# Token-major projections: 512 columns at a time and a bank per token tile, in place of 256 columns and a bank per pair of tiles

## The chip, the cores and the metric

The kernel runs on one core of a Trainium2 chip. The metric is the time of one execution on the device, in microseconds (us); a kernel's time is the median of several runs. PE is the matrix engine, DVE the vector engine, ACT the scalar engine, SP the engine that issues most of the loads, and PEld PE's weight loads. PSUM, where PE writes, has eight banks of 128 partitions x 512 fp32.

## The reference, cut to what matters

Two layers of a block over 256 context tokens and 256 image tokens (512 in all), model width 1024. Each layer projects the normalized input into many parts, mixes them in three branches, and ends in a convolutional FFN. The last layer needs only the image tokens, except in keys and values. The parts that the change touches:

```python
# every layer, h is the normalized, modulated input [tokens, 1024]
q_x = rope_axial(rms_norm(bq_x.reshape(b, n, 4, 2, 64), q_norm_g), ang_r, ang_c)   # 512 columns
k_x = rope_axial(rms_norm(bk_x ...), ang_r, ang_c)                                 # 512 columns
k_c = rms_norm(bk_c ...)                                                           # context: no rotation
v   = bv                                                                           # 512 columns

def spatial_gating(u, v, norm_g, w_s, b_s):                                        # sv: 512 columns
    u = gelu(u)
    v = rms_norm(gelu(v).reshape(b, n // 128, 128, 4, 128), norm_g)
    mixed = einsum('gij,bnjgc->bnigc', w_s, v) + b_s.T[:, :, None]
    return u * mixed.reshape(b, n, 512)
```

Beside them stands a gated delta rule (a triangular solve per chunk of 64 tokens and a scan over the chunks), softmax attention with the difference of two maps, three gated branch products and the FFN.

## The kernel before, in words

Products are made from fp32 operands split in two (`hh`/`hl` for the input, `wh`/`wl` for the weights): three matmuls per 128 rows of the contraction. Most projections are feature-major (`proj_fm`): weights stationary, 512 tokens (256 in layer 1) streaming. Four are token-major (`proj_tm`, line 706): 128 tokens of the input are stationary and the weights' columns stream, so the tokens land on the partitions, where norms over a head's columns are a reduction along the free axis. These four are attention's v, k and q and the gate's sv.

In `proj_tm` each of the four has two groups of 256 columns. A PSUM bank holds a pair of token tiles, 256 columns each. Two banks of tag "p" hold the two pairs of 512 tokens; in layer 1, q and the gate work on the image tokens alone, one pair. For each of two weight blocks (512 KB: 512 contraction rows x 256 columns, line 711) the loop goes over pairs, the two tiles of a pair, four steps of the contraction and three matmuls. Then `use` runs for every pair.

`use_qk` (line 755) reads a pair out of PSUM with ACT (`axq`), squares it (`asq`), sums the squares per head on DVE (`qkss`), takes a reciprocal root in nine small DVE steps (`rsqrt`, line 242), multiplies by the gain or, for image tokens, by the cosines, and adds the swapped halves times the sines (four small multiplications, line 776), multiplies k by its root, transposes four 128x128 blocks on PE into a bank of tag "a" (`pqkT`, line 789) and copies the result to `kT` or `qT` with ACT. `axq`, `asq` and `axc` share three buffers of tag "ta". `sgu`'s `use` (line 676) does Gelu, square, sum and root, and leaves the mixing product (`mix`, line 687) to be issued later, by `flush` in the next projection. `v` is only copied.

PSUM banks by tag: "p" 2, "g" 3, "a" 2, "b" 1. Weights are loaded by SP into three buffers `wr` of 512 KB, split by ACT (`wh`) and DVE (`wl`) into four buffers each of 128x512. `more` (line 478) takes one step of the modulation vectors of later stages: a 512 KB load into a single buffer `wmt` and, in layer 0, two products with a running sum on DVE (line 471). Layer 0's `attn_project` takes one such step ahead of each of its six groups.

The order of instructions on each engine is fixed when the kernel is built, by a planner: it goes through time with its own costs and gives each engine the ready instruction of highest priority, which is program order, except that work under `high_priority` goes ahead of the rest. So the delta rule's keys, solve, intra products and scan (lines 579 to 587), and in layer 0 the `use` of q and k, go ahead of matmuls that are only there to be done; these fill PE between them. Each engine then runs its own list in order. Buffers and banks of a tag go to its tiles in the order of the program.

In `mixer` (line 574) the order is: delta rule's q, k, v and gates; its keys; the solve (`gdn_solve`, line 1149: 31 steps of two dependent DVE operations, `sT` and `sL`, then products on PE, `pZ` and `pU`, and ACT's copies into `U`); `attn_project`; the scan; `sgu`; z; the attention core; the branches.

Of the kernel before, what the change touches and what calls it, by code (L numbers as in the profile page):

```python
# [14 lines left out]
AF = mybir.ActivationFunctionType  # L15
ALU = mybir.AluOpType
# [3 lines left out]
L = 2  # L20
# [75 lines left out]
def host_layout(i):  # L96
    i = {k: np.asarray(v) for k, v in i.items()}
    f = np.ascontiguousarray
    o = {}
# [7 lines left out]
    w = i["w_in"]  # L107
# [38 lines left out]
    for name, key in (("alog", "a_log"), ("dtb", "dt_bias")):  # L146
        a = i[key]
# [26 lines left out]
class _Kernel:  # L174
# [488 lines left out]
    def sgu(self):  # L663
        nc, l, c0 = self.nc, self.l, self.c0
        gu = self.slot(10, "gu", [128, 4, NT])
        for m in range(4):
            p = self.bank("p", "pu")
            self.proj_fm(self.a["wfm"][l, 16 + m], 8, self.hh, self.hl, c0, p)
            self.more(l == 0)
            self.act(gu[:, m, c0:], p[:, :NT - c0], AF.Gelu_apprx_tanh)  # L670
        wb = self.tp.tile([128, 2, 4, 128], F32, tag="gS", name="sguwb", bufs=1)
        wT, bs = wb[:, 0], wb[:, 1]
        nc.scalar.dma_start(out=wT, in_=self.a["sguw"][l])
        nc.scalar.dma_start(out=bs, in_=self.a["sgub"][l].rearrange("p (g i) -> p g i", g=4))

        def use(gr, t0, p):
            gv = self.tmp("gv", [128, 2, 2, 128])
            self.act(gv, p.rearrange("p (t g c) -> p t g c", t=2, g=2), AF.Gelu_apprx_tanh)
            sq = self.tmp("gsq", [128, 2, 2, 128])
            self.act(sq, gv, AF.Square)  # L680
            ss = self.small("gss", [128, 2, 2], bufs=2)
            nc.vector.tensor_reduce(out=ss, in_=sq, axis=AX.X, op=ALU.add)
            self.rsqrt(ss, ss, 1.0 / 128, EPS, "s")
            self.mul(gv, gv, ss.unsqueeze(3).to_broadcast([128, 2, 2, 128]))
            self.late.append(lambda: mix(gr, t0, gv))

        def mix(gr, t0, gv):
            pm = self.bank("g", "pmix")
            pv = pm.rearrange("p (g t i) -> p g t i", g=2, t=2)
            for t in range(2):  # L690
                for g in range(2):
                    self.mm(pv[:, g, t], gv[:, t, g, :], wT[:, 2 * gr + g, :])
            for g in range(2):
                G = 2 * gr + g
                mx = self.tmp("mx", [128, 2, 128])
                self.stt(mx, pv[:, g], self.P(l, "sg", G), bs[:, G].unsqueeze(1).to_broadcast([128, 2, 128]),
                         ALU.mult, ALU.add)
                d = gu[:, G, t0 * 128:t0 * 128 + 256].rearrange("p (t i) -> p t i", t=2)
                self.mul(d, d, mx)

        for gr in range(2):
            self.proj_tm(6 + gr, c0, lambda t0, p, gr=gr: use(gr, t0, p))
        self.dump(f"ya{l}", gu)
        return gu

    def proj_tm(self, g, c0, use, ahead=False):

        pairs = range(c0 // 256, 2)
        pt = {i: self.bank("p", f"ptm{i}") for i in pairs}
        for kb in range(2):  # L710
            wh, wl = self.wblock(self.a["wtm"][self.l, g, kb].rearrange("p k m -> p (k m)"), 1024, 512)
# [12 lines left out]
        with ExitStack() as es:  # L724
            if ahead:
                es.enter_context(self.tc.high_priority(offset=AHEAD))
            for i in pairs:
                use(2 * i, pt[i])

    def flush(self):  # L730

# [4 lines left out]
    def attn_project(self):  # L736
        nc, l, c0 = self.nc, self.l, self.c0
        tabs = {}
        for nm in ("q", "k"):
            g = self.P(l, nm + "g")  # L740
            ct = self.small(f"ct{nm}", [128, 2, 64])
            st = self.small(f"st{nm}", [128, 2, 64])
# [12 lines left out]
        def use_qk(nm, dstT, gr):  # L755
            g, ct, st = tabs[nm]

            def use(t0, p):
                p8 = self.tmp("axq", [128, 2, 4, 64], tag="ta", bufs=3)
                self.act(p8, p.rearrange("p (t h d) -> p t h d", t=2, d=64), AF.Copy)  # L760
                sq = self.tmp("asq", [128, 2, 4, 64], tag="ta", bufs=3)
                self.act(sq, p8, AF.Square)
                ss = self.small("qkss", [128, 2, 4], bufs=2)
                nc.vector.tensor_reduce(out=ss, in_=sq, axis=AX.X, op=ALU.add)
                rs = self.small("qkrs", [128, 2, 4], bufs=2)
                self.rsqrt(rs, ss, 1.0 / 64, EPS, "q")
                xc = self.tmp("axc", [128, 2, 4, 64], tag="ta", bufs=3)
                if t0 == 0:
                    self.mul(xc, p8, g.unsqueeze(1).unsqueeze(1).to_broadcast([128, 2, 4, 64]))
                else:  # L770
                    xs = sq
                    self.mul(xc, p8, ct.unsqueeze(2).to_broadcast([128, 2, 4, 64]))
                    p5 = p8.rearrange("p t h (a b f) -> p t h a b f", a=2, b=2, f=16)
                    x5 = xs.rearrange("p t h (a b f) -> p t h a b f", a=2, b=2)
                    s5 = st.rearrange("p t (a b f) -> p t a b f", a=2, b=2)
                    for t in range(2):
                        for b in range(2):
                            self.mul(x5[:, t, :, :, b, :], p5[:, t, :, :, 1 - b, :],
                                     s5[:, t, :, b, :].unsqueeze(1).to_broadcast([128, 4, 2, 16]))
                    self.add(xc, xc, xs)  # L780
                if nm == "k":
                    self.mul(xc, xc, rs.unsqueeze(3).to_broadcast([128, 2, 4, 64]))
                else:
                    nc.vector.tensor_scalar_mul(self.qscale[:, t0:t0 + 2, 4 * gr:4 * gr + 4], rs, 0.125)
                pt = self.bank("a", "pqkT")
                pv = pt.rearrange("p (h t) -> p h t", h=2)
                for h in range(2):
                    for t in range(2):
                        nc.tensor.transpose(pv[:, h, 128 * t:128 * t + 128],
                                            xc[:, t, 2 * h:2 * h + 2, :].rearrange("p m d -> p (m d)"),  # L790
                                            self.C("ident"))
                self.act(dstT[:, 2 * gr:2 * gr + 2, 128 * t0:128 * t0 + 256], pv, AF.Copy)

            return use

        def one(w):
            gr = w % 2
            if w < 2:
                self.proj_tm(w, 0, use_qk("k", kT, gr), l == 0)
            elif w < 4:  # L800
                self.proj_tm(w, 0, lambda t0, p, gr=gr: self.act(
                    vB[:, t0:t0 + 2, 256 * gr:256 * gr + 256], p.rearrange("p (t c) -> p t c", t=2), AF.Copy))
            else:
                self.proj_tm(w, c0, use_qk("q", qT, gr), l == 0)
# [580 lines left out]
```

## Time and profile before

| | |
|---|---|
| median of 3 runs | 1648.79 us (1646.63 to 1651.72) |
| the profiled execution | 1647.11 us, span 1645.3 us |
| PE busy | 1585.5 us (96%) |
| DVE busy | 1201.7 us (73%) |
| ACT busy | 763.0 us (46%) |
| granted PE clock, mean | 0.982 |

The profile is that of one execution. The span runs from the first to the last instruction; busy time of PE includes the overlap of matmuls in its pipeline. The chain of work that ended last goes back from the last instruction to what released it, step by step; a long unbroken run of matmuls in it shows how far apart their starts are.

### The profile page before, as it was taken

To read this page: it belongs to the slowest core of one execution; us is meant where nothing else is said; L and a number is where in the kernel's file an instruction comes from. 1 tells how busy PE (TensorE), PEld (TensorE's weight loads), DVE (VectorE), ACT (ScalarE), POOL (GpSimd) and SP (SyncE) were. 2 spreads that over 40 slices of the span, in tenths; PEclk is the share of its full clock that TensorE was granted. 3 is DMA by queue.
4 is the path that set the end of the run, shared out by engine and by line. 5 is a ranking of instruction groups with operands and counts; after the bars stand their busy time and mean duration, and the time that the engine had idled before them with its cause. 6 is when DMAs were issued, how large, how long until landed. Compare 5 with 4: busy or idle time off the path is not lost.

```text
span 1645.3 us, 27181 instructions
## 1 busy us (share of the span) xinstructions
PE 1585.5 (96%) x10478; PEld 1339.4 (81%) x10478; DVE 1201.7 (73%) x2793; ACT 763.0 (46%) x1451; POOL 6.6 (0%) x16
## 2 busy tenths in 40 slices
PE   5999999999999998999999998999999999989999
PEld 3778977876788886888788887788878799989999
DVE  5648977788764456888778886659767866788685
ACT  3644461156532333544224442664723764566564
POOL 0000000000000000000000000000000000000000
PEclk9989999999999999999999999999999999999999
DMA  8413311142343433355556665222222246645655
GB/s 335 135 54 105 118 65 52 64 122 73 99 145 96 148 96 97 116 160 161 173 185 200 196 200 201 66 90 56 75 65 78 93 130 218 191 141 180 191 181 154
DMA packets 65282, 218.21 MB, mean 133 GB/s; under 512 B 7552, under 2 KB 13696, under 8 KB 63232
## 3 DMA queue, kind: packets, MB, share of 16 engines
q1 hardware_dynamic: 63280, 208.70, 40.2%
q10 hardware_dynamic: 1872, 7.77, 1.3%
q8 instruction: 82, 1.34, 0.3%
q14 instruction: 48, 0.39, 0.1%
HBM read 213.29 MB, written 3.15 MB: 132 GB/s over the span
## 4 chain that ended last, share of the span: by engine, by line
PE 78%; DVE 9%; DMA 4%; ACT 4%; issue 3%; ACTq 0%; DVEq 0%
PE pup L240 16%; PE pg L240 12%; PE pdn L240 11%; PE pqkv L240 8%; PE pbr L240 6%; PE pwo L240 4%; PE ptm L240 4%; DMA wmt<-in_wmt_dram 3%; PE pu L240 2%; PE psc L240 2%; PE pj L240 2%; PE pS L240 2%; ACT U L237 1%; PE pkS L240 1%; PE po L240 1%
## 5 line engine op out<-in xcount | busy, mean ns | idle before, releaser
L237 ACT ACTIVATE wh<-wr 128x512 fp32r<-128x512 f32 (+1 forms) x594 | 365.6, 621 | 411.2 <-PE pdn L240 84.1
L219 DVE TENSOR_TENSOR wl<-wr,wh 128x512 fp32r<-128x512 f32 (+1 forms) x592 | 399.2, 680 | 155.8 <-ACT wh L237 153.0
L240 PE MATMUL pup<-hh,wh 128*128 128x512 f32 (+1 forms) x704 | 238.4, 339 | 3.0 <-ACT hh L237 2.8
L240 PE MATMUL pup<-hh,wl 128*128 128x512 f32 (+1 forms) x704 | 238.2, 338 | 0.0
L240 PE MATMUL pup<-hl,wh 128*128 128x512 f32 (+1 forms) x704 | 237.4, 338 | 0.0
L240 PEld LDWEIGHTS pup<-hh,wh 128*128 128x128 f32 x704 | 134.9, 192 | 18.0 <-ACT hh L237 3.4
L240 PEld LDWEIGHTS pup<-hh,wl 128*128 128x128 f32 x704 | 134.9, 192 | 13.8
L240 PEld LDWEIGHTS pup<-hl,wh 128*128 128x128 f32 x704 | 134.6, 192 | 14.1
L240 PE MATMUL pg<-hh,wh 128*128 128x512 f32 (+1 forms) x384 | 131.0, 341 | 0.1
L240 PE MATMUL pg<-hh,wl 128*128 128x512 f32 (+1 forms) x384 | 130.4, 340 | 0.1
L240 PE MATMUL ptm<-wh,hl 128*128 128x256 f32 x448 | 130.4, 291 | 0.0
L240 PE MATMUL pg<-hl,wh 128*128 128x512 f32 (+1 forms) x384 | 130.3, 339 | 0.0
L240 PE MATMUL ptm<-wl,hh 128*128 128x256 f32 x448 | 129.9, 290 | 0.3 <-DVE wl L219 0.3
L240 PE MATMUL ptm<-wh,hh 128*128 128x256 f32 x448 | 129.6, 289 | 0.0
L471 DVE SCALAR_TENSOR_TENSOR wmt<-wmt,scb 128x1024 f32<-128x1024 f32 x80 | 97.6, 1220 | 34.0 <-DMA wmt<-in_wmt_dram 33.6
L234 DVE SCALAR_TENSOR_TENSOR fcv<-pup,par,fcv 128x510 f32<-128x510 f32 (+1 forms) x176 | 107.3, 611 | 18.5 <-ACT fcv L237 18.4
L240 PE MATMUL pdn<-fl,wh 128*128 128x512 f32 (+1 forms) x352 | 118.1, 336 | 1.2 <-DVE fl L219 1.2
L240 PE MATMUL pdn<-fh,wh 128*128 128x512 f32 (+1 forms) x352 | 118.6, 337 | 0.7 <-ACT fh L237 0.7
L240 PE MATMUL pdn<-fh,wl 128*128 128x512 f32 (+1 forms) x352 | 118.3, 336 | 0.0
L240 PEld LDWEIGHTS ptm<-wl,hh 128*128 128x128 f32 x448 | 86.7, 194 | 2.5 <-issue 1.7
L240 PEld LDWEIGHTS ptm<-wh,hh 128*128 128x128 f32 x448 | 86.5, 193 | 2.7 <-issue 2.0
L240 PEld LDWEIGHTS ptm<-wh,hl 128*128 128x128 f32 x448 | 86.6, 193 | 2.1 <-issue 1.7
(332 smaller groups left out, 3182.0 us busy)
## 6 DMA issues: line engine op xcount, KB each, us to landing
wmt<-in_wmt_dram SPq DMA_DIRECT2D x80, 512.0 KB, 3.6
wr<-in_wup_dram SPq DMA_DIRECT2D x80, 512.0 KB, 3.9
wr<-in_wfm_dram SPq DMA_DIRECT2D x78, 512.0 KB, 3.6
wr<-in_wtm_dram SPq DMA_DIRECT2D x32, 512.0 KB, 3.6
wr<-in_wdn_dram SPq DMA_DIRECT2D x32, 512.0 KB, 4.0
wr<-in_wbr_dram SPq DMA_DIRECT2D x24, 512.0 KB, 3.6
wm<-in_wmod_dram SPq DMA_DIRECT2D x8, 1024.0 KB, 10.9
wr<-in_wo_dram SPq DMA_DIRECT2D x16, 512.0 KB, 3.8
```

What stands on the lines that cost most here:

```text
L219: self.nc.vector.tensor_tensor(out=out, in0=a, in1=b, op=op)
L234: self.nc.vector.scalar_tensor_tensor(out=out, in0=a, scalar=s, in1=b, op0=op0, op1=op1)
L237: self.nc.scalar.activation(out, a, f, bias=bias, scale=scale, **k)
L240: self.nc.tensor.matmul(out, lhsT, rhs, start=start, stop=stop, **k)
L471: nc.vector.scalar_tensor_tensor(out=o, in0=w, scalar=1.0, in1=sb[:, v], op0=ALU.mult, op1=ALU.mult, accum_out=m4[:, n % 4, v:v + 1])
```

## The change

`proj_tm` takes all 512 columns of a projection at once: four groups in a layer instead of eight, each matmul 512 columns wide, a bank per tile of 128 tokens. With four tiles, tiles 0 and 1 take the banks of "p", tiles 2 and 3 those of "a"; with two tiles, both take "p" or both "a", by a counter. The weights are laid out anew: a block of 512 KB holds 256 contraction rows x 512 columns, so there are four blocks in a group. `use` runs per token tile, on 512 columns of one tile instead of 256 columns of two. The transposes of q and k go to the bank of tag "b". The gate's normed values of all tiles are kept, and a mixing product is issued for every second tile. The squares of the gate take a buffer of tag "tg". Layer 0's six modulation steps come in pairs ahead of the three groups v, k, q.

```diff
-    o["wtm"] = f(tm.reshape(L, 2, 4, 128, 8, 256).transpose(0, 4, 1, 3, 2, 5))
+    o["wtm"] = f(tm.reshape(L, 4, 2, 128, 4, 512).transpose(0, 4, 1, 3, 2, 5))
...
+    def two(self, name):
+        return [self.bank("a", name) for _ in range(2)]
...
-        def use(gr, t0, p):
-            gv = self.tmp("gv", [128, 2, 2, 128])
...
+        gvs = {}
+
+        def use(t, p):
+            gvs[t] = gv = self.tmp("gv", [128, 4, 128])
...
+            sq = self.tmp("gsq", [128, 4, 128], tag="tg", bufs=4)
...
-            self.late.append(lambda: mix(gr, t0, gv))
+            if t % 2:
+                self.late.append(lambda: mix(t - 1))
...
-        for gr in range(2):
-            self.proj_tm(6 + gr, c0, lambda t0, p, gr=gr: use(gr, t0, p))
+        self.proj_tm(3, c0, use)
...
-        pairs = range(c0 // 256, 2)
-        pt = {i: self.bank("p", f"ptm{i}") for i in pairs}
-        for kb in range(2):
+        ts = range(c0 // 128, 4)
+        self.alt += 1
+        pt = {}
+        for t in ts:
+            if len(ts) == 4 and t >= 2 or len(ts) == 2 and self.alt % 2:
+                if t == 2:
+                    pa = self.two("ptm")
+                pt[t] = pa[t - 2]
+            else:
+                pt[t] = self.bank("p", "ptm")
+        for kb in range(4):
             wh, wl = self.wblock(self.a["wtm"][self.l, g, kb].rearrange("p k m -> p (k m)"), 1024, 512)
-            for i in pairs:
-                for tt in range(2):
-                    o = pt[i][:, 256 * tt:256 * tt + 256]
-                    xs = slice((2 * i + tt) * 128, (2 * i + tt) * 128 + 128)
-                    for kk in range(4):
-                        k = kb * 4 + kk
-                        j, ws = kk // 2, slice(kk % 2 * 256, kk % 2 * 256 + 256)
-                        f = k == 0 and tt == 0
-                        self.mm(o, self.hh[:, k, xs], wh[j][:, ws], start=f, stop=False, skip_group_check=True)
-                        self.mm(o, self.hl[:, k, xs], wh[j][:, ws], start=False, stop=False, skip_group_check=True)
-                        self.mm(o, self.hh[:, k, xs], wl[j][:, ws], start=False, stop=k == 7, skip_group_check=True)
+            for t in ts:
+                xs = slice(128 * t, 128 * t + 128)
+                for kk in range(2):
+                    k = kb * 2 + kk
+                    self.mm(pt[t], self.hh[:, k, xs], wh[kk], start=k == 0, stop=False)
+                    self.mm(pt[t], self.hl[:, k, xs], wh[kk], start=False, stop=False)
+                    self.mm(pt[t], self.hh[:, k, xs], wl[kk], start=False, stop=k == 7)
...
-                    for t in range(2):
-                        for b in range(2):
-                            self.mul(x5[:, t, :, :, b, :], p5[:, t, :, :, 1 - b, :],
-                                     s5[:, t, :, b, :].unsqueeze(1).to_broadcast([128, 4, 2, 16]))
+                    for b in range(2):
+                        self.mul(x5[:, :, :, b, :], p5[:, :, :, 1 - b, :],
+                                 s5[:, :, b, :].unsqueeze(1).to_broadcast([128, 8, 2, 16]))
...
-                pt = self.bank("a", "pqkT")
...
+                pt = self.bank("b", "pqkT")
...
-        for w in (2, 0, 3, 1, 4, 5):
-            self.more(l == 0)
+        for w in (1, 0, 2):
             one(w)
```

In `one`, layer 0 now begins with `self.more(2)`; group 1 is v, 0 is k, 2 is q.

## Rows read from the trace of the kernel before

**Rows 1.** The page: busy us (share of the span) xinstructions

```profile
PE 1585.5 (96%) x10478; PEld 1339.4 (81%) x10478; DVE 1201.7 (73%) x2793; ACT 763.0 (46%) x1451; POOL 6.6 (0%) x16
```

**Rows 2.** Windows: start:end, us, busy of each engine, PEclk, DMA share, GB/s

```profile
118.00:220.00 102.00, 99.92 (x991) 90.85 (x990) 92.07 (x276) 51.12 (x84) 2.07 (x4) 0.97 0.32 101
...
450.00:602.00 152.00, 152.00 (x674) 125.86 (x673) 78.89 (x129) 50.68 (x86) 0.00 (x0) 1.00 0.39 125
...
1098.00:1187.00 89.00, 84.67 (x872) 76.78 (x871) 71.87 (x225) 49.48 (x79) 2.07 (x4) 0.96 0.22 66
```

**Rows 3.** PE's waits, 118 to 226, then 1098 to 1190: us, times, longest

```profile
PE pgram L240 <- ACT U L237: 2.6, 1, 2.6
...
PE pkv L1035 <- ACT U L237: 2.3, 2, 1.9
```

**Rows 4.** Groups by form, PE: one of three ptm kinds, busy, mean ns

```profile
L240 PE MATMUL ptm<-wh,hl 128*128 128x256 f32 x448 | 130.4, 291 | 0.0
```

**Rows 5.** The chain that ended last, in order of time: start, us, what

```profile
97.02 11.13 PE pqkv L240 x48
...
315.50 15.09 PE ptm L240 x124
...
601.81 43.53 PE pwo L240 x192
...
1546.83 63.36 PE pup L240 x528
```

**Rows 6.** By tile, asq then gu: ns min/median/max, first and last start

```profile
L219 DVE TENSOR_TENSOR asq<-axq,stk x16: 278/284/295, 163.3 to 1169.2; 128x128 f32<-128x128 f32 x16
...
L219 DVE TENSOR_TENSOR gu<-gu,mx x12: 415/418/421, 332.7 to 1285.8; 128x256 f32<-128x256 f32 x12
```

**Rows 7.** Timeline of ACT near 157 us: start, us, what, idle before

```profile
156.64 0.60 ACT L237 ACTIVATE axq<-ptm 128x512 f32<-128x512 f32 x1 [2.37 <-PE ptm L240]
```

**Rows 8.** By tile, wmt, 118 to 226 us

```profile
L471 DVE SCALAR_TENSOR_TENSOR mj<-wmt,scb x8: 1161/1218/1229, 117.8 to 218.5; 128x1024 bf16<-128x1024 f32 x8
...
  DMA wmt<-in_wmt_dram: 3.0, 2
...
DMA to landing us min/median/max: 3.5/3.7/4.6
```

**Rows 9.** Windows of tile ptm alone: PE, PEld, ACT, PEclk, DMA, GB/s

```profile
118.00:152.00 34.00, 18.47 (x132) 16.72 (x132) 1.18 (x2) 1.00 0.30 100
...
1098.00:1127.00 29.00, 13.82 (x97) 12.12 (x98) 0.60 (x1) 1.00 0.13 37
```

**Rows 10.** Timeline of PE, 160 to 217 us: the first two sets of transposes

```profile
166.35 0.66 PE L789 MATMUL pqkT<-cst,axc 128*128 128x128 f32 x4 [0.30 <-DVE axc L219]
...
175.98 0.66 PE L789 MATMUL pqkT<-cst,axc 128*128 128x128 f32 x4
```

**Rows 11.** Timeline of DVE, 163 to 169 us

```profile
163.35 0.29 DVE L219 TENSOR_TENSOR asq<-axq,stk 128x128 f32<-128x128 f32 x1
163.55 0.27 DVE L219 TENSOR_TENSOR sL<-sL,sT 128x112 f32<-128x112 f32 x1
...
168.41 0.68 DVE L219 TENSOR_TENSOR axc<-axc,asq 128x512 f32<-128x512 f32 x1
```

**Rows 12.** By tile, sL: the solve's products, both layers

```profile
L219 DVE TENSOR_TENSOR sT<-sX,sL x62: 181/359/426, 158.4 to 1168.3; 128x31 f32<-128x31 f32 x4, 128x60 f32<-128x60 f32 x4, 128x87 f32<-128x87 f32 x4, 128x112 f32<-128x112 f32 x4
```

**Rows 13.** Windows: layer 1, behind the solve (columns as in rows 2)

```profile
1170.00:1187.00 17.00, 15.08 (x305) 14.23 (x304) 10.34 (x34) 16.73 (x23) 2.07 (x4) 0.80 0.20 64
```

**Rows 14.** Timeline of PE: the first and last of ten ptm matmuls

```profile
1180.96 0.41 PE L240 MATMUL ptm<-wl,hh 128*128 128x256 f32 x1
...
1182.88 0.35 PE L240 MATMUL ptm<-wl,hh 128*128 128x256 f32 x1
```

**Rows 15.** Timeline of DVE: the solve's last step (layer 0), its first (layer 1)

```profile
207.44 0.18 DVE L219 TENSOR_TENSOR sL<-sL,sT 128x31 f32<-128x31 f32 x1
...
1132.38 0.18 DVE L219 TENSOR_TENSOR sT<-sX,sL 128x31 f32<-128x31 f32 x1
```

More of the change, by code (lines that the diff above doesn't have):

```diff
@@ L674, in sgu @@
         nc.scalar.dma_start(out=bs, in_=self.a["sgub"][l].rearrange("p (g i) -> p g i", g=4))
[L676 to L679 removed]
+        gvs = {}
+        def use(t, p):
+            gvs[t] = gv = self.tmp("gv", [128, 4, 128])
+            self.act(gv, p.rearrange("p (g c) -> p g c", g=4), AF.Gelu_apprx_tanh)
+            sq = self.tmp("gsq", [128, 4, 128], tag="tg", bufs=4)
@@ L680, in use @@
             self.act(sq, gv, AF.Square)
-            ss = self.small("gss", [128, 2, 2], bufs=2)
+            ss = self.small("gss", [128, 4], bufs=2)
             nc.vector.tensor_reduce(out=ss, in_=sq, axis=AX.X, op=ALU.add)
             self.rsqrt(ss, ss, 1.0 / 128, EPS, "s")
-            self.mul(gv, gv, ss.unsqueeze(3).to_broadcast([128, 2, 2, 128]))
-            self.late.append(lambda: mix(gr, t0, gv))
-        def mix(gr, t0, gv):
-            pm = self.bank("g", "pmix")
-            pv = pm.rearrange("p (g t i) -> p g t i", g=2, t=2)
-            for t in range(2):
-                for g in range(2):
[L692 to L699, printed above, removed]
@@ L701, in sgu, with mix @@
-        for gr in range(2):
-            self.proj_tm(6 + gr, c0, lambda t0, p, gr=gr: use(gr, t0, p))
+            self.mul(gv, gv, ss.unsqueeze(2).to_broadcast([128, 4, 128]))
+            if t % 2:
+                self.late.append(lambda: mix(t - 1))
+        def mix(t0):
+            for gr in range(2):
+                pm = self.bank("g", "pmix")
+                pv = pm.rearrange("p (g t i) -> p g t i", g=2, t=2)
+                for t in range(2):
+                    for g in range(2):
+                        self.mm(pv[:, g, t], gvs[t0 + t][:, 2 * gr + g, :], wT[:, 2 * gr + g, :])
+                for g in range(2):
+                    G = 2 * gr + g
+                    mx = self.tmp("mx", [128, 2, 128])
+                    self.stt(mx, pv[:, g], self.P(l, "sg", G), bs[:, G].unsqueeze(1).to_broadcast([128, 2, 128]),
+                             ALU.mult, ALU.add)
+                    d = gu[:, G, t0 * 128:t0 * 128 + 256].rearrange("p (t i) -> p t i", t=2)
+                    self.mul(d, d, mx)
@@ L726, in proj_tm @@
                 es.enter_context(self.tc.high_priority(offset=AHEAD))
-            for i in pairs:
-                use(2 * i, pt[i])
+            for t in ts:
+                use(t, pt[t])
     def flush(self):
@@ L753, in attn_project, with use_qk, use @@
         self.qscale = self.small("qscale", [128, 4, 8])
-        def use_qk(nm, dstT, gr):
+        def use_qk(nm, dstT):
             g, ct, st = tabs[nm]
[L758 to L761, printed above, removed]
+            def use(t, p):
+                p8 = self.tmp("axq", [128, 8, 64], tag="ta", bufs=3)
+                self.act(p8, p.rearrange("p (h d) -> p h d", d=64), AF.Copy)
+                sq = self.tmp("asq", [128, 8, 64], tag="ta", bufs=3)
@@ L762, in use @@
                 self.act(sq, p8, AF.Square)
-                ss = self.small("qkss", [128, 2, 4], bufs=2)
+                ss = self.small("qkss", [128, 8], bufs=2)
                 nc.vector.tensor_reduce(out=ss, in_=sq, axis=AX.X, op=ALU.add)
-                rs = self.small("qkrs", [128, 2, 4], bufs=2)
+                rs = self.small("qkrs", [128, 8], bufs=2)
                 self.rsqrt(rs, ss, 1.0 / 64, EPS, "q")
-                xc = self.tmp("axc", [128, 2, 4, 64], tag="ta", bufs=3)
-                if t0 == 0:
-                    self.mul(xc, p8, g.unsqueeze(1).unsqueeze(1).to_broadcast([128, 2, 4, 64]))
+                xc = self.tmp("axc", [128, 8, 64], tag="ta", bufs=3)
@@ L770, in use @@
+                if t < 2:
+                    self.mul(xc, p8, g.unsqueeze(1).to_broadcast([128, 8, 64]))
                 else:
                     xs = sq
[L772 to L776, printed above, removed]
-                        for b in range(2):
-                            self.mul(x5[:, t, :, :, b, :], p5[:, t, :, :, 1 - b, :],
-                                     s5[:, t, :, b, :].unsqueeze(1).to_broadcast([128, 4, 2, 16]))
+                    self.mul(xc, p8, ct[:, t - 2].unsqueeze(1).to_broadcast([128, 8, 64]))
+                    p5 = p8.rearrange("p h (a b f) -> p h a b f", a=2, b=2, f=16)
+                    x5 = xs.rearrange("p h (a b f) -> p h a b f", a=2, b=2)
+                    s5 = st[:, t - 2].rearrange("p (a b f) -> p a b f", a=2, b=2)
+                    for b in range(2):
+                        self.mul(x5[:, :, :, b, :], p5[:, :, :, 1 - b, :],
+                                 s5[:, :, b, :].unsqueeze(1).to_broadcast([128, 8, 2, 16]))
@@ L780, in use @@
                     self.add(xc, xc, xs)
                 if nm == "k":
-                    self.mul(xc, xc, rs.unsqueeze(3).to_broadcast([128, 2, 4, 64]))
+                    self.mul(xc, xc, rs.unsqueeze(2).to_broadcast([128, 8, 64]))
                 else:
-                    nc.vector.tensor_scalar_mul(self.qscale[:, t0:t0 + 2, 4 * gr:4 * gr + 4], rs, 0.125)
-                pt = self.bank("a", "pqkT")
[L786 to L791, printed above, removed]
@@ L792, in use @@
-                self.act(dstT[:, 2 * gr:2 * gr + 2, 128 * t0:128 * t0 + 256], pv, AF.Copy)
+                    nc.vector.tensor_scalar_mul(self.qscale[:, t, :], rs, 0.125)
+                pt = self.bank("b", "pqkT")
+                for h in range(4):
+                    nc.tensor.transpose(pt[:, 128 * h:128 * h + 128],
+                                        xc[:, 2 * h:2 * h + 2, :].rearrange("p m d -> p (m d)"), self.C("ident"))
+                self.act(dstT[:, :, 128 * t:128 * t + 128], pt.rearrange("p (h t) -> p h t", h=4), AF.Copy)
@@ L794, in use_qk @@
             return use
         def one(w):
[L797 to L802, printed above, removed]
-            else:
-                self.proj_tm(w, c0, use_qk("q", qT, gr), l == 0)
-        for w in (2, 0, 3, 1, 4, 5):
-            self.more(l == 0)
+            if l == 0:
+                self.more(2)
@@ L808, in attn_project @@
+            if w == 0:
+                self.proj_tm(0, 0, use_qk("k", kT), l == 0)
+            elif w == 1:
+                self.proj_tm(1, 0, lambda t, p: self.act(vB[:, t, :], p, AF.Copy))
+            else:
+                self.proj_tm(2, c0, use_qk("q", qT), l == 0)
+        for w in (1, 0, 2):
             one(w)
```

## The prediction, made before the changed kernel was run

> **What bounds the kernel now.** Read the page's busy shares first: PE is busy for 96% of the span, DVE for 73% [rows 1]. Then three stretches: layer 0's projections with the solve beside them, its branches, and layer 1's projections [rows 2]. PE is busy for 99.9 of 102 us, 152 of 152 and 84.7 of 89. So up to the first layer's FFN, PE's own work sets the end, and what is taken from PE or added as PE idling there shows nearly one for one. In layer 0's projections DVE is almost full too (92.1 of 102), and that matters below. PE's waits in the two projection stretches are few: the longest is 2.6 us in layer 0 and 1.9 in layer 1, both for ACT's copies of U, the end of the triangular solve [rows 3]. All edits are in these stretches and in the gating work around the scan.
>
> **Columns.** There are 1344 matmuls of 256 columns today (three kinds of 448 each, of which the first stands in [rows 4]); they become 672 of 512 columns. The listed duration of one is no cost, since matmuls overlap; the cost is the distance between starts, read from long unbroken runs in the chain [rows 5]. 256 columns: 63.36 us / 528 = 120.0 ns (pup, layer 1); ptm itself 15.09 / 124 = 121.7. 512 columns: 43.53 / 192 = 226.7 ns (pwo), and in the busy first stage 11.13 / 48 = 231.9 (pqkv). Taken: 1344 x 120.0 = 161.3 us against 672 x 226.7 = 152.3, so 9.0 us less of PE. From both sides: 121.7 against 226.7 gives 11.2, 120.0 against 231.9 gives 5.4.
>
> The Trainium skill (TensorE: Matmul & The Clock Gate, section "Back-to-back issue gap") speaks against this: it gives columns / 2.4 GHz + 2.5 ns for a warm gap. By it two matmuls of 256 take 218.3 ns and one of 512 takes 215.8, an estimated saving of 1.7 us in all. This trace doesn't agree for 256 columns, which stand 120.0 ns apart and not 109.2.
>
> **Work per token tile.** There are as many uses as before (14 for q and k, 6 for the gate), each of 128x512, so Copy, Square, the reduction, the small reciprocal-root steps, the multiplications, the four transposes and the copy back are the same in number and size. Only the rotation's swap changes: 32 multiplications of 128x128 at 0.284 us become 16 of 128x256; the nearest row of that size takes 0.418 [rows 6]. DVE gives up 9.1 - 6.7 = 2.4 us. DVE isn't last in these stretches as a whole, so I take 0 for the end; at most 2.4. The transposes' result moves from two banks to one: a next use comes over 4 us later, a copy takes 0.60 [rows 7], so the wait is hidden; 0, at most 14 x 0.60 = 8.4 if nothing hid it. The gate's four tiles have three buffers in layer 0, so the fourth waits for the first mixing, which stands behind z's first projection (24 x 226.7 ns = 5.4 us); it holds only one bank of the scores, and z's projections lie beside it: 0, at most 5.4.
>
> **Loads and modulation steps.** Weight loads stay 32 of 512 KB. Six modulation steps in layer 0's projections stay six, but come in pairs before four weight loads. One buffer serves them, so the second load waits on SP for DVE's two products of the first (2 x 1.22 us) and takes 3.7 us to land [rows 8]; the group's four weight loads are queued behind it on SP. Three weight buffers of some 5.4 us of PE each stand ahead, so PE doesn't see it: 0. DVE already stood 3.0 us for two such landings [rows 8]; three pairs could cost it 3 x 3.7 = 11.1, no gain below 0. I take 0, since others' work is there to be put between.
>
> **The new wait.** The order becomes v, k, q, and four tiles take all of banks p, p, a, a. q's tile 3 can't start until k's tile 3 has been read out, and that copy needs a "ta" buffer; there are three, and they are passed on at the pace of DVE's work on the tiles before. Behind it stand PE's remaining matmuls of q, since their weights' buffers (4) are held too.
> - When: by 152 us PE has done 132 ptm matmuls [rows 9], 15.8 us at 120.0 ns. So of v's 96 x 226.7 = 21.8 us some 6 are left, v ends near 158 and k near 179.7; k's tile 0 is complete at 175.6, and q reaches tile 3 18 matmuls after k's end, at 183.8.
> - Readout: today k's first use takes 9.7 us from its copy (156.64) to the first transpose (166.35), the second use's transpose is at 175.98 [rows 7, 10], because the solve's steps stand between the use's steps on DVE [rows 11]. The second use will have no rotation (4 x 0.29 + 0.68 us, and as many solve steps fewer): some 15 us after the first copy instead of 19.3. Then 0.68 + 2 x 0.42 of the third use and 0.60 of copy: the bank is free at 175.6 + 15 + 2.1 = 192.7.
> - PE has other work until then if the planner puts it in: the next block of tiles 0 to 2 (18 x 226.7 ns = 4.1 us) and two sets of transposes (2 x 0.66). So 192.7 - 183.8 - 5.4 = 3.5 us idle. Ends: 0 if DVE goes as if without a solve, 8.9 without filling.
> - Layer 1: the solve starts at 1132.4 [rows 15] and its steps, 62 in a layer, take about 0.36 each [rows 12], 22 us; with no k use beside it until k's tile 0 (1127 + 10 + 17.7 = near 1155, from 97 ptm matmuls by 1127 [rows 9]) it is almost through then. q's two tiles both take "a" banks there. The first waits for k's tile 2, some 2 us; the second is covered by the solve's products on PE. Taken 2.0, ends 0 and 6.
>
> **The clock.** After the solve's small matmuls the granted clock is 0.80 over 1170 to 1187 us [rows 13], and ten ptm matmuls in a row, from 1180.96 to 1182.88, stand 0.21 us apart instead of 0.12 [rows 14]: its lower level, 1.2 GHz instead of 2.4, costs 1.92 - 9 x 0.12 = 0.8 us there. An idle PE in front of q can bring that once more: 1.0, ends 0 and 2 (one in each layer).
>
> **What goes.** In layer 0 the k uses come after the larger part of the solve instead of beside it. Some two to four uses at about 2.5 to 4 us of DVE leave its way (the solve's last step is at 207.4 [rows 15]), so U comes some 8 us earlier, while PE is there about as late as now. The 2.6 us wait goes. Layer 1's 1.9 I leave.
>
> **Sum.** -9.0 - 2.6 + 3.5 + 2.0 + 1.0 = -5.1 us. The profiled execution took 1647.1 (span 1645.3, 1.8 around it), 1.7 below the median of 1648.8; so 1642.0 for such an execution and 1643.7 as a median. Some 5 us (0.3%) is what a measurement of this kernel can tell from no change.
>
> **Rivals.**
> - The waits are hidden: the uses run faster once the solve is through, or the planner finds cover. For it: DVE is full today only because of both together [rows 2]. Against: three buffers are a fixed chain. -9.0 - 2.6 gives 1637.2. Chance 0.24.
> - Slower: the bank of k's tile 3. If PE's order has nothing in the gap, 8.9 in layer 0, 6 in layer 1 and 2 x 1.0 of clock stand against 9.0: +8, 1656.7. It decides from the point where the two waits pass 9 us together. For it: the contended pace in the trace [rows 7, 10]; against: PE's order elsewhere is well filled [rows 3]. Chance 0.17.
> - The columns bring less: 512 columns run at 231.9 as in the first stage: -5.4 - 2.6 + 6.5 = -1.5, 1647.3. For it: the same DVE and ACT load; against: pwo and pup. Chance 0.09.
> - A pair costs almost what one large matmul does: if the 256s stood only 2.5 ns per pair above, 1.7 - 2.6 + 6.5 gives +2.2, 1651.0. The runs in rows 5 show 13 ns. Chance 0.03. (That is the page's rule above.)
> - The paired modulation steps stall DVE for 11 us, half of it reaching U: 1649. Chance 0.05.
>
> **Numbers.** The forecast has 0.42, own range 1638 to 1650 (bank waits 0 to 12, columns 5.4 to 11.2). Faster by over 0.3% means below 1643.8: half of the forecast and almost all of the first rival, 0.44. Slower, above 1653.8: most of the second rival and a little of the rest, 0.19. Between: 0.37. The range for 8 in 10 is 1633 to 1657.
>
> **What would show it.** ptm matmuls 512 wide, 227 ns apart in unbroken runs: the columns. A PE gap of 3 to 4 us near 185 to 193, ended by ACT's copy of ptm, in layer 0, and a shorter one in layer 1: the bank. The solve's last step in layer 0 well before 207, and no wait for U. wl or weight loads ending PE's waits would make the loads' step wrong. The forecast is wrong if the ptm gaps pass 10 us, or if there are none.

## The result, and the profile after

The changed kernel takes 1663.74 us (median of 4 runs, 1660.29 to 1665.72) where the kernel before took 1648.12 beside it (4 runs): ratio 1.0091, 95% interval 1.0076 to 1.0106. It is slower by 15.6 us. The prediction said 1643.7, between 1633 and 1657: wrong in sign, and outside its range. The profiled execution took 1665.72 us, its span 1663.9.

The page's busy times, as in [rows 1]:

```profile
PE 1589.8 (96%) x9806; PEld 1305.6 (78%) x9806; DVE 1209.8 (73%) x2777; ACT 767.1 (46%) x1451; POOL 6.6 (0%) x16
```

There are 672 matmuls fewer, yet PE is busy for 4.3 us longer, not shorter. The chain of waits in order of time (start, us, what) shows that the wide matmuls themselves are nearly as cheap as forecast: an unbroken run of 55 takes 12.71 us, 231 ns each, where the forecast took pwo's 226.7 and allowed 231.9 [rows 5].

```profile
327.54 12.71 PE ptm L243 x55
618.65 43.53 PE pwo L243 x192
```

So where did the time go? Cut at the first product of the delta rule's gates (pba) and the first of the output projection (pwo) of each layer, the two profiled executions compare as follows (us, from those starts in the traces):

| stretch | before | after |
|---|---|---|
| start to layer 0's pba | 114.9 | 117.0 |
| layer 0: pba to pwo (all edits of this layer) | 486.7 | 501.5 |
| layer 0's rest, up to layer 1's pba | 492.8 | 491.1 |
| layer 1: pba to pwo | 325.2 | 328.5 |
| rest | 225.7 | 225.8 |

Layer 0 loses 14.8 us and layer 1 3.3, where both should have gained from the columns. The stretches that no edit touches differ by about 2 us between executions, so no stretch is read closer than that here. Windows of layer 0, counted from its pba (60 to 80, 80 to 95, 95 to 110, 110 to 130 us), first of the kernel before (columns as in [rows 2]):

```profile
174.90:194.90 20.00, 19.53 (x163) 19.15 (x162) 19.65 (x61) 7.82 (x14) 0.00 (x0) 1.00 0.43 133
194.90:209.90 15.00, 14.82 (x129) 14.32 (x129) 15.00 (x60) 8.26 (x13) 0.00 (x0) 1.00 0.23 72
209.90:224.90 15.00, 12.81 (x283) 11.53 (x279) 6.93 (x21) 13.29 (x18) 2.07 (x4) 0.77 0.20 72
224.90:244.90 20.00, 19.43 (x211) 14.24 (x213) 17.83 (x43) 11.23 (x21) 0.00 (x0) 1.00 0.24 79
```

and the same four of the changed kernel:

```profile
177.00:197.00 20.00, 15.61 (x62) 11.80 (x60) 19.28 (x57) 5.47 (x10) 0.00 (x0) 0.91 0.39 125
197.00:212.00 15.00, 8.98 (x28) 6.75 (x28) 12.64 (x49) 4.95 (x8) 0.00 (x0) 0.66 0.12 36
212.00:227.00 15.00, 14.94 (x290) 13.07 (x291) 8.89 (x20) 11.58 (x13) 2.07 (x4) 0.77 0.44 143
227.00:247.00 20.00, 17.10 (x154) 12.42 (x153) 12.56 (x33) 14.68 (x27) 0.00 (x0) 0.91 0.00 1
```

PE idles 13.4 us in the four windows instead of 3.4, and its granted clock falls to 0.91 and 0.66 in the first two, where it had been 1.00. PE's waits over the whole run (us in total, times, longest) name the cause:

```profile
PE pkv L1040 <- ACT U L240: 7.4, 2, 6.9
PE ptm L243 <- ACT axq L240: 6.9, 3, 2.9
...
PE pqkT L796 <- DVE axc L222: 5.2, 1, 5.2
...
PE pgram L243 <- ACT U L240: 2.9, 1, 2.9
```

The second line is new: q's matmuls wait for ACT's readout of k's tiles. The third stands in the same chain. The first grew from 1.9 at the longest [rows 3]. The timeline of ACT in layer 0 (start, us, what, idle before and what ended it) shows the four readouts of k and the first two copies of its transposes:

```profile
177.77 0.60 ACT L240 ACTIVATE axq<-ptm 128x512 f32<-128x512 f32 x1 [0.52 <-PE ptm L243]
...
182.33 0.60 ACT L240 ACTIVATE axq<-ptm 128x512 f32<-128x512 f32 x1 [3.30 <-DVE qkss L774]
...
186.91 0.60 ACT L240 ACTIVATE axq<-ptm 128x512 f32<-128x512 f32 x1 [1.89 <-DVE axc L222]
194.69 0.60 ACT L240 ACTIVATE akT<-pqkT 128x512 f32<-128x512 f32 x1 [7.19 <-PE pqkT L796]
...
200.98 0.60 ACT L240 ACTIVATE akT<-pqkT 128x512 f32<-128x512 f32 x1 [5.17 <-PE pqkT L796]
202.25 0.60 ACT L240 ACTIVATE axq<-ptm 128x512 f32<-128x512 f32 x1 [0.67 <-DVE axc L222]
```

In the last weight block PE finishes a tile every 1.36 us (6 x 0.227), so all four tiles of k are in PSUM by about 182; the fourth readout starts at 202.25, 24.5 us after the first. ACT is idle ahead of the last three until DVE is done with a step of an earlier tile: the "ta" buffers are late. DVE's timeline over the same time shows why it is slow:

```profile
178.23 1.22 DVE L474 SCALAR_TENSOR_TENSOR wmt<-wmt,scb 128x1024 f32<-128x1024 f32 x1
...
183.57 1.22 DVE L474 SCALAR_TENSOR_TENSOR mj<-wmt,scb 128x1024 bf16<-128x1024 f32 x1
...
185.72 0.41 DVE L222 TENSOR_TENSOR sT<-sX,sL 128x256 f32<-128x256 f32 x1
...
189.17 1.22 DVE L474 SCALAR_TENSOR_TENSOR wmt<-wmt,scb 128x1024 f32<-128x1024 f32 x1
...
191.60 0.69 DVE L222 TENSOR_TENSOR axc<-axc,qkrs 128x512 f32<-128x512 f32 x1
...
194.76 1.23 DVE L474 SCALAR_TENSOR_TENSOR mj<-wmt,scb 128x1024 bf16<-128x1024 f32 x1 [0.72 <-DMA wmt<-in_wmt_dram]
...
199.03 0.69 DVE L222 TENSOR_TENSOR axc<-axc,qkrs 128x512 f32<-128x512 f32 x1
```

Four products of the modulation steps (1.22 us each, plus 0.08 for their sum) stand between k's first readout and its second product with the root at 199.03, among the solve's steps. These are at their widest there, 256 columns in 0.41 us (185.72); beside k's first use in the kernel before they were narrower, 112 columns in 0.27 [rows 11]. Grouped by tile (count, then ns and first and last start), these products number 6 + 5 beside the solve (157 to 214 us):

```profile
L474 DVE SCALAR_TENSOR_TENSOR wmt<-wmt,scb x6: 1216/1220/1225, 157.9 to 200.0; 128x1024 f32<-128x1024 f32 x6
...
L474 DVE SCALAR_TENSOR_TENSOR mj<-wmt,scb x5: 1218/1224/1226, 162.8 to 194.8; 128x1024 bf16<-128x1024 f32 x5
```

and 3 + 2 in the kernel before (155 to 208 us):

```profile
L471 DVE SCALAR_TENSOR_TENSOR mj<-wmt,scb x3: 1216/1226/1229, 170.3 to 201.4; 128x1024 bf16<-128x1024 f32 x3
...
L471 DVE SCALAR_TENSOR_TENSOR wmt<-wmt,scb x2: 1217/1220/1222, 171.8 to 178.5; 128x1024 f32<-128x1024 f32 x2
```

And this is what PE does meanwhile (its timeline):

```profile
187.56 0.50 PE L243 MATMUL ptm<-wh,hh 128*128 128x512 f32 x1 [2.05 <-ACT axq L240]
...
188.60 0.63 PE L243 MATMUL ptm<-wh,hh 128*128 128x512 f32 x1
189.03 0.63 PE L243 MATMUL ptm<-wh,hl 128*128 128x512 f32 x1
...
194.06 0.60 PE L796 MATMUL pqkT<-cst,axc 128*128 128x128 f32 x4
199.86 1.09 PE L796 MATMUL pqkT<-cst,axc 128*128 128x128 f32 x4 [5.20 <-DVE axc L222]
202.89 0.80 PE L243 MATMUL ptm<-wh,hh 128*128 128x512 f32 x1 [1.95 <-ACT axq L240]
```

PE stops at k's third bank (2.05), at its transposes (5.20) and at k's fourth bank (1.95). Behind the first and the last gap the matmuls stand 0.43 us apart (188.60, 189.03) and not 0.227. The granted clock was 0.51 from 188.00 to 191.20 and 0.50 from 203.00 to 208.50: its lower level, 1.2 GHz, after an idle PE.

In layer 1 the same bank meets the end of the solve. ACT's timeline there:

```profile
1176.72 0.60 ACT L240 ACTIVATE axq<-ptm 128x512 f32<-128x512 f32 x1 [0.71 <-DVE axc L222]
...
1187.44 2.18 ACT L240 ACTIVATE U<-sLC 32x512 f32<-32x512 f32 x2
...
1196.12 3.09 ACT L240 ACTIVATE U<-pU 32x256 f32<-32x256 f32 x8
...
1203.01 0.59 ACT L240 ACTIVATE axq<-ptm 128x512 f32<-128x512 f32 x1
```

and PE's:

```profile
1177.38 0.50 PE L243 MATMUL ptm<-wh,hh 128*128 128x512 f32 x1 [2.92 <-ACT axq L240]
...
1197.70 1.11 PE L1040 MATMUL pkv<-cst,vT 128*128 128x128 f32 x4 [6.91 <-ACT U L240]
```

k's fourth readout stands behind ACT's copies into U, so q's second tile can't be computed while PE waits for U: the work that used to cover that wait is itself held by the bank. PE idles 6.9 us instead of 1.9.

### The profile page after: what moved, and what is told of

Read it like the earlier page. It is cut to its first block, busy times and chain, and to the rows that moved or that the text cites. A ratio compares the mean times of both kernels' runs of the same rounds, so it can differ in the third digit from the quotient of the medians.

```text
span 1663.9 us, 25840 instructions
## 1 busy us (share of the span) xinstructions
PE 1589.8 (96%) x9806; PEld 1305.6 (78%) x9806; DVE 1209.8 (73%) x2777; ACT 767.1 (46%) x1451; POOL 6.6 (0%) x16
## 4 chain that ended last, share of the span: by engine, by line
PE 79%; DVE 9%; DMA 4%; ACT 3%; issue 3%; ACTq 0%; DVEq 0%
PE pup L243 16%; PE pg L243 11%; PE pdn L243 11%; PE pqkv L243 8%; PE pbr L243 6%; PE ptm L243 4%; PE pwo L243 4%; DMA wmt<-in_wmt_dram 4%; PE pu L243 2%; PE psc L243 2%; PE pS L243 2%; ACT U L240 1%; PE pj L243 1%; DVE wl L222 1%; PE po L243 1%
## 5 line engine op out<-in xcount | busy, mean ns | idle before, releaser
L243 PE MATMUL ptm<-wh,hh 128*128 128x512 f32 x224 | 92.9, 415 | 6.9 <-ACT axq L240 6.9
L243 PE MATMUL ptm<-wl,hh 128*128 128x512 f32 x224 | 91.0, 411 | 1.3 <-DVE wl L222 1.3
L243 PE MATMUL ptm<-wh,hl 128*128 128x512 f32 x224 | 92.0, 411 | 0.0
L243 PE MATMUL pqkv<-hh,wh 128*128 128x512 f32 (+1 forms) x192 | 76.4, 399 | 6.7 <-ACT hh L240 4.7
L243 PEld LDWEIGHTS pg<-hh,wh 128*128 128x128 f32 x384 | 72.9, 190 | 11.6 <-issue 3.3
L243 PEld LDWEIGHTS pg<-hh,wl 128*128 128x128 f32 x384 | 72.8, 190 | 10.0 <-DVE wl L222 1.6
```

Source lines behind the costliest of these rows:

```text
L243: self.nc.tensor.matmul(out, lhsT, rhs, start=start, stop=stop, **k)
```

## The experiments

Ratios are to the kernel before, run on the same chip beside each (its medians 1647.7 to 1648.6). A difference between two experiments is taken between their medians.

**Is it the buffers that hold the banks?** k's readouts get four buffers of their own (the tag "go" is free at that time); all else as changed.

```diff
-                p8 = self.tmp("axq", [128, 8, 64], tag="ta", bufs=3)
+                p8 = self.tmp("axq", [128, 8, 64], **(dict(tag="go", bufs=4) if nm == "k" else dict(tag="ta", bufs=3)))
```

> The changed kernel, with k's copy out of PSUM (axq) in four buffers of its own (those of the scan's output, free at that time) instead of three shared with the squares and products. Theory bank (q's tiles wait for k's banks, read out at DVE's pace; PE idles, its clock drops): PE's waits for axq, 6.9 us, fall below 1, the 5.2 us wait of the second transposes and layer 1's 6.9 us wait for U shrink with them, and some 4 us of low clock go: 13 to 17 us less than the changed kernel, 1647 to 1651. Rival steps (the paired modulation steps load DVE beside the solve): the solve still ends near 213 us, and no more than 4 us are won, 1659 to 1663. Rival columns (512 columns bring nothing here): 1656 to 1660, since only the waits go that were added.

1646.55 us, ratio 0.9988 (0.9979 to 0.9997): 17.2 us less than the changed kernel, more than its whole loss. Layer 0 takes 489.4 us (501.5 in the changed kernel), layer 1 324.6 (328.5). ACT's timeline in layer 0 of this version, k's first and last readout, and PE's waits in layer 1:

```profile
176.56 0.60 ACT L240 ACTIVATE axq<-ptm 128x512 f32<-128x512 f32 x1 [0.15 <-PE ptm L243]
...
184.17 0.58 ACT L240 ACTIVATE axq<-ptm 128x512 f32<-128x512 f32 x1
```

```profile
PE pkv L1040 <- ACT U L240: 2.6, 2, 2.4
PE ptm L243 <- ACT axq L240: 1.2, 1, 1.2
```

The fourth readout now comes 7.6 us after the first, and the wait for U is back at 2.4. The solve is no faster for it: its last step still comes 96.8 us after pba (96.5 in the changed kernel). So the loss is PE's wait for the banks, not the solve.

The control: the same edit in the kernel before.

> The kernel before, with one edit alone: k's readouts take the four buffers of tag "go" in place of the three of "ta". Theory (the buffers cost only where a bank hangs on them; in the kernel before q's first pair of banks is free long before PE comes to it, and no wait of PE there is ended by a readout): 1648, within 2 us of the kernel before. Rival (three buffers are too few in either kernel, and the 17.2 us that the same edit brought to the changed kernel are a gain of its own): 5 us or more below the kernel before.

1648.92 us, ratio 1.0008 (0.9999 to 1.0017): no gain. The buffers cost only where a bank hangs on them.

**Do the paired modulation steps cost anything?** One step ahead of the first and of the third weight block of each group, as many in all, in place of pairs.

```diff
+            if self.l == 0 and g < 3 and kb % 2 == 0:
+                self.more()
...
-            if l == 0:
-                self.more(2)
```

> The changed kernel, with layer 0's six modulation steps taken one at a time (ahead of the first and the third weight block of v, k and q) instead of in pairs. Theory bank: the waits for axq stay, and the time falls by at most 4 us, 1659 to 1664. Rival steps: of eleven products of these steps that DVE makes beside the solve only about five stay, the solve's last step comes 6 to 8 us earlier (near 206), and the time falls by 8 to 12 us, 1651 to 1656.

1657.48 us, ratio 1.0051 (1.0038 to 1.0064): 6.3 less than the changed kernel, between the two ranges. The solve ends 87.6 us after pba instead of 96.5, but nine of the eleven products still stand beside it, not five. Over the whole run the waits for axq take 5.8 us (6.9 in the changed kernel) and those of pkv for U 7.6 (7.4). ACT's first and last readout of k in layer 0, and PE's second transposes:

```profile
175.74 0.58 ACT L240 ACTIVATE axq<-ptm 128x512 f32<-128x512 f32 x1
...
197.96 0.60 ACT L240 ACTIVATE axq<-ptm 128x512 f32<-128x512 f32 x1 [1.21 <-DVE axc L222]
```

```profile
195.03 1.09 PE L798 MATMUL pqkT<-cst,axc 128*128 128x128 f32 x4 [5.04 <-DVE axc L222]
```

The fourth readout comes 22.2 us after the first instead of 24.5, and PE's waits for k's banks and transposes in layer 0 are 8.9 us instead of 9.2: the chain is long without pairs too. Layer 0, where the edit is, takes 498.1 us in this profiled execution (501.5), 3.4 of the 6.3. How the pairs cost the rest is not shown. Pairs in the kernel before, ahead of three of its six groups:

```diff
-            self.more(l == 0)
+            if l == 0 and w in (2, 3, 4):
+                self.more(2)
```

> The kernel before, with the six modulation steps in three pairs (ahead of the first, third and fifth group) and nothing else changed. Theory bank: no bank waits here, so 0 to 3 us slower than before, 1648 to 1651. Rival steps: the solve ends 5 us or more later and the time rises by 6 to 10 us, 1654 to 1658.

1647.85 us, ratio 0.9993 (0.9984 to 1.0002): nothing. Both edits together on the changed kernel, k's four buffers and single steps:

> Both edits: k's copy out of PSUM in four buffers of its own, and the modulation steps one at a time. If the two costs are separate (bank waits 17 us, steps 6), they add up: 1638 to 1642, some 7 us under the kernel before. If the steps cost only by making the readouts later, nothing is left of their 6 us once the readouts are free: 1645 to 1648. Layer 0's solve should end near 88 us after the gates' product instead of 97 in either case.

1645.30 us, ratio 0.9983 (0.9974 to 0.9992): 1.25 below the version with four buffers alone, less than the uncertainty, so the two costs don't add up. The solve's last step comes 91.6 us after pba and not near 88. So the pairs cost 6.3 us where k's readouts hold banks, too little to tell from nothing where they don't, and nothing in the kernel before.

**What are the columns worth?** Each matmul of 512 columns as two of 256, in the changed kernel and then in the version of 1645.30.

```diff
-                    self.mm(pt[t], self.hh[:, k, xs], wh[kk], start=k == 0, stop=False)
+                    for c in range(2):
+                        cs = slice(256 * c, 256 * c + 256)
+                        self.mm(pt[t][:, cs], self.hh[:, k, xs], wh[kk][:, cs], start=k == 0 and c == 0, stop=False,
+                                skip_group_check=True)
...
```

> The changed kernel with its banks, buffers, order and steps, but every matmul of 512 columns issued as two of 256. This prices the columns alone. If the columns bring what the prediction took (9.0 us of PE, PE setting the end), the time rises by 5 to 11 us over the changed kernel, 1669 to 1675. Rival columns (PE waits for readouts anyway, so narrower matmuls only fill the waits): within 3 us of the changed kernel, 1661 to 1667.

1664.63 us, ratio 1.0094 (1.008 to 1.0109): 0.9 more than the changed kernel, less than its uncertainty. PE's waits are shorter instead: over the whole run those for axq fell from 6.9 to 3.0 us, those of pkv for U from 7.4 to 4.8.

> As the run with both edits, but every matmul of 512 columns issued as two of 256: the price of the columns where PE no longer waits for readouts. If PE sets the end here, 5 to 9 us above the run with both edits (9.0 us by the distances of the starts, of which layer 0's part is 5). If DVE's chain (solve, U, scan) still sets it, within 3 us of it, as the same edit did in the changed kernel (0.9 us).

1651.65 us, ratio 1.0025 (1.0016 to 1.0033): 6.35 us more than with 512 columns, good to some 2 us by the two intervals. The columns are worth 9.4 ns a pair (6.35 us / 672) where k's readouts hold no bank, and next to nothing where PE then waits for DVE.

The Trainium skill (TensorE: Matmul & The Clock Gate, section "Back-to-back issue gap") gives N / 2.4 + 2.5 ns as the warm gap of an isolated matmul of N columns; an estimate from it makes a pair 2.5 ns dearer than one of 512. These two runs don't agree with it.

**What does the order do?** First the kernel before with v's groups together and then k's.

```diff
-        for w in (2, 0, 3, 1, 4, 5):
+        for w in (2, 3, 0, 1, 4, 5):
```

> The kernel before, with its six groups in the order v v k k q q instead of v k v k q q, nothing else changed: the order of the changed kernel with 256 columns and two banks. Theory bank: four uses of k in a row meet the same three buffers, PE waits 3 to 8 us for axq, and the time is 3 to 8 us above before, 1651 to 1656. Rival (the order doesn't matter, the wait comes from the four banks of the new form alone): within 2 us of before.

1656.27 us, ratio 1.0046 (1.0033 to 1.0059): 8.4 us slower from the order alone. The theory's time was nearly right and its mechanism was not: PE has no wait for axq here. Layer 1 takes 328.7 us (325.2 before), with a wait for U of 3.7; layer 0 488.6 (486.7), and the start of this execution was 3.3 longer, which the order can't explain by itself. Then, in the version of 1645.30, k first:

```diff
-        for w in (1, 0, 2):
+        for w in (0, 1, 2):
```

> As the run with both edits, with the groups in the order k, v, q instead of v, k, q. Then 22 us of v's matmuls, which ask nothing of DVE, stand between k's and q's, and k's work on DVE stands beside the delta rule's keys and the early solve. If the uses of k and q in a row are what is left of the loss: 3 to 6 us under the run with both edits. If that work only delays the solve: its end moves 5 us or more, and the time is 0 to 5 us above it.

1657.03 us, ratio 1.0059 (1.0045 to 1.0073): 11.7 more, where at most 5 were expected. The solve ends later in both layers (95.8 and 80.8 us after pba, where the version of 1645.30 had 91.6 and 70.7), and layer 1 takes 329.6 us with waits for U of 5.4. k's work beside the early solve slows the solve. The other way round, k last:

```diff
-        for w in (1, 0, 2):
+        for w in (1, 2, 0):
```

> The changed kernel with k's readouts in four buffers of their own and single modulation steps (1645.3 so far), in the order v, q, k in place of v, k, q. Theory (a projection that stands behind one whose tiles are read out through the three buffers "ta" beside the solve waits for their banks): now q is that one, its four readouts go at the pace of the solve, k's tile 3 waits for q's tile 3 as q's did for k's in the changed kernel: 5 to 12 us longer, 1650 to 1657, with a wait of PE for q's axq in layer 0. Rival (it is the keys' own work, their scaling and early transposes, that crowds DVE beside the solve, and late keys free it): 1641 to 1645, the solve's last step in layer 0 sooner than 91 us after its gates' first product.

1642.40 us, ratio 0.9974 (0.9964 to 0.9984), the fastest of all. The theory of this run failed: q's four tiles were expected to be as late through "ta" as k's. Their readouts start at 178.75, 181.60, 184.40 and 189.49, the last 10.7 us after the first. The rival, that k's own work crowds DVE, gave the time, and the solve's last step (89.5 us after pba, under its 91). This version is below both kernels; against the two that stand next, 1644.5 and 1645.3, the intervals overlap. The same order in the changed kernel, with nothing else altered (three buffers, paired steps), tells which of its edits did it:

> The changed kernel with nothing but its order altered: v, q, k in place of v, k, q; the three buffers "ta" and the paired modulation steps stay. Theory (the bank wait hangs on k's own chain: its product with the reciprocal root and its transposes hold "ta"; q's tiles, whose axc needs no root, pass through the three buffers in some 11 us, as they did with the version of 1642.4): no wait of PE for axq in layer 0 beyond 1 us, 1643 to 1650, 13 us or more below the changed kernel's 1663.7. Rival (what the version of 1642.4 gains is its four buffers and single steps, and with paired steps and three buffers q's tiles are as late as k's were): 1655 or more, with PE waiting 3 us or more for axq in layer 0.

1644.54 us, ratio 0.9982 (0.997 to 0.9995): 19.2 us less than the changed kernel, from the order of two projections. The profiled execution is the slowest of the eleven (1651.31). PE's waits in layer 0 (118 to 345 us), and ACT's first and last readout of q and then of k:

```profile
PE pqkT L796 <- DVE axc L222: 2.7, 1, 2.7
PE pgram L243 <- ACT U L240: 2.5, 1, 2.5
```

```profile
177.31 0.60 ACT L240 ACTIVATE axq<-ptm 128x512 f32<-128x512 f32 x1 [0.20 <-PE ptm L243]
...
192.33 0.60 ACT L240 ACTIVATE axq<-ptm 128x512 f32<-128x512 f32 x1 [2.63 <-DVE asq L222]
...
205.75 0.60 ACT L240 ACTIVATE axq<-ptm 128x512 f32<-128x512 f32 x1 [0.95 <-PE ptm L243]
...
237.17 0.59 ACT L240 ACTIVATE axq<-ptm 128x512 f32<-128x512 f32 x1
```

q's tiles pass in 15.0 us, since their axc needs no root: their first transposes, for which PE waits 2.7 us, come 5.8 us after the first readout (183.15), where k's in the changed kernel came after 16.3. k's tiles still take 31.4 us, and no wait of PE in layer 0 is ended by their readouts. The bank is late only for whoever comes next. Last, the version of 1645.30 with q's readouts in "go" too:

```diff
-                p8 = self.tmp("axq", [128, 8, 64], **(dict(tag="go", bufs=4) if nm == "k" else dict(tag="ta", bufs=3)))
+                p8 = self.tmp("axq", [128, 8, 64], tag="go", bufs=4)
```

> The changed kernel with single modulation steps, and the readouts of k and of q in the four buffers of "go" (only k's had them in the version of 1645.3). Theory (behind q's tiles no projection of the same stretch waits for a bank, so its readouts are nobody's bound; four buffers for eight uses are still enough for k's four): 1645.3 within 2 us. Rival (what still separates layer 0 from the kernel before is that q's uses hold "ta" back): 2 to 4 us shorter, 1641 to 1643.5, and PE's wait for axc gone.

1649.85 us, ratio 1.001 (0.9999 to 1.0021), its twelve runs between 1643.6 and 1655.0: 4.55 above the version of 1645.30 and outside both ranges. Neither that nor its spread is explained.

## Why the prediction was wrong

**The step that failed** is the readout in the part on the new wait: "some 15 us after the first copy", and from it the bank free 17.1 us after k's tile 0 (175.6 to 192.7). The place, the releaser and the order of events were right. Measured from the first readout (177.77), the first transposes came after 16.3 us (194.06) instead of 9.7, the second after 22.1 (199.86) instead of 15, and the bank was free after 25.1 (the copy of 202.25 takes 0.60). So nearly all of the miss lies in the first use, whose 9.7 us were read where the solve had just begun [rows 7, 10]. By the starts of DVE's instructions, those 9.7 us (156.64 to 166.35) hold 3.3 us of the solve's steps and no product of the modulation steps (the first stands at 170.3). The 16.3 us hold 5.9 us of the solve's steps, about as many but at their widest, and 3.6 us of such products. The use itself and the split of the weights take nearly the same in both (6.4 and 6.7).

The forecast put k's uses "after the larger part of the solve". Its own rows have the solve's products from 158.4 [rows 12] to 207.4 [rows 15] in layer 0, and its k's tile 0, at 175.6, stands in the first half of that. It also had the products, and priced them apart. That they come in pairs is the smaller part of it: with single steps the last readout still starts 22.2 us after the first. Four buffers take the whole effect of the chain away (17.2 us).

**Its other terms.**
- Columns, -9.0 (ends -5.4 and -11.2): -6.35 where k's readouts hold no bank, so within the ends and nearer the small one. In the changed kernel it was -0.9, since time saved on PE ahead of a wait only lengthens the wait.
- Layer 0's wait, +3.5 (0 to 8.9): PE's idle time grew by 10.0 us over the four windows. Two of k's banks made PE wait, not one, and the matmuls that were to fill the gap (4.1 us) ran before the transposes, whose wait of 5.2 stands ahead of the rest in PE's order.
- Layer 1's wait, +2.0 (0 to 6): 2.9 for k's third bank, and the longest wait for U from 1.9 to 6.9, because the work that covered it hung on k's fourth bank. "The second is covered by the solve's products" failed.
- Clock, +1.0 (0 to 2): in layer 0, 7 gaps from 188.18 to 191.16 and 12 from 202.89 to 208.18 between matmuls, in layer 1 another 7 from 1177.95 to 1180.94. At 0.227 us each these 26 would take 5.9 us; they took 11.3. So 5.4 us, beyond its end also without the 0.8 that the kernel before had in layer 1 [rows 14].
- The solve "some 8 us earlier" in layer 0: its last step came 96.5 us after pba instead of 92.5, and the wait for U stayed (2.9 for 2.6). All four uses of k begin before that step, and eleven modulation products stand beside the solve in place of five. How much of the delay is theirs is not shown: with nine of them (single steps) it ended 87.6 us after pba.
- Paired steps, 0: 6.3 us while banks hung on DVE. The rival of 1649 put its price on U; with single steps the wait for U in layer 0 fell from 2.9 to 1.9 us, so U is part of it and the rest is open.
- For the rotation's DVE work, the single bank of the transposes and the gate's fourth buffer, 0: no wait in the traces speaks against it; none was tried by itself.

The rival that came nearest was the slower one: the bank of k's tile 3, deciding once the two waits pass 9 us together. With the transposes' wait they did. Its time was 1656.7, its chance 0.17. The forecast's own test ("wrong if the ptm gaps pass 10 us") was met if the transposes' wait in the same chain is counted: 2.05 + 5.20 + 1.95 in layer 0 and 2.92 in layer 1 make 12.1.

**What stays open.** In layer 0, idle time (+10.0), clock (+4.0 of the 5.4) and columns (384 x 13.3 ns = -5.1, by the prediction's price) make +8.9 of the measured 14.8; what is left, 5.9, is more than the 2 us by which untouched stretches vary, and no run gives it a name. With the columns at the measured 9.4 ns (-3.6) and the lower clock of the fourth window (0.91 where it had been 1.00, at most 20 x 0.09 = 1.8 us) it would be 2.6. Nor is it shown why bunching v ahead of k costs the kernel before 8.4 us, of which its layers show 5.4. The changed kernel has that order too. With four buffers it is only 2.0 us below the kernel before, where the columns alone bring 6.35, so some of the order's cost may still be in it, and no run separates that.

## What to carry to other kernels

When tiles take more banks, follow each bank to the operation that frees it, and that one to the buffer it needs, and count everything the pacing engine has in between at the time when the chain will run, not when it ran before: here a solve at its widest steps, and what another part of the same change puts there. Ask who uses the bank next: swapping two projections took away all of the loss, and no wait of PE in layer 0 was then ended by the slow chain's readouts. A saving on PE ahead of a wait is next to no saving (0.9 us of 6.35). An edit that costs nothing in one kernel (the pairs in the kernel before) can cost in another, where a bank hangs on the engine that it loads (6.3 us).

## What was not expected of the hardware

How dear a short gap of PE is. Behind an idle PE of 2.05 us (before 187.56) and one of 2.92 us (before 1177.38) the matmuls stood 0.43 us apart, the lower of the two levels (granted clock 0.51 from 188.00 to 191.20 and 0.50 from 1178.00 to 1181.00), for about 3 us each time: 7 gaps of 0.43 in place of 0.227 us, another 1.4 us that the wait's own row does not show.
